# A hybrid encoder trunk: two gate blocks between the first two differential heads, and convolution taps dealt out differently

## The chip, the cores and the metric

The kernel runs on one core of a Trainium2 chip. The metric is the device time of one execution in microseconds (us); the median of several runs is given. The profile and the trace come from one further execution.

The engines go by short names: PE is TensorE (matrix products, with PEld for its weight loads), DVE is VectorE, ACT is ScalarE, POOL is GpSimd, SP is SyncE, which here only issues DMAs (copies between memories). SBUF is the working memory with 128 partitions, PSUM the memory into which PE writes.

## The reference

Two layers (DEPTH 2) over 512 tokens of width 1024, in float32. A layer computes three token mixers side by side from one normed input, merges them by gates, and goes on with a gated feed-forward part and a gated per-layer input:

```
h = rmsnorm(x, norm_mix[i])
proj = h @ w_in[i]
qa, ka, va, glu_in, qc, kc, vc, gates = split(proj)
ya = diff_attention(qa, ka, va, ...)          # 4 heads, two softmaxes each, rope on q and k
yb = conformer_conv(glu_in, ...)              # GLU, 31 taps per channel, layernorm, silu
yc = neighbourhood_attention(qc, kc, vc, rpb) # 8 heads, 8 x 16 window on an 8 x 64 grid
ga, gb, gc = split(sigmoid(gates))
merged = ga * (ya @ w_br_a[i]) + gb * (yb @ w_br_b[i]) + gc * (yc @ w_br_c[i])
x = x + merged @ w_o[i]
...                                           # feed-forward part, per-layer input
```

The convolution is one of 31 taps per channel over 512 channels, without mixing of channels: for each of four groups of 128 channels, 31 multiply-adds over a tile of 128 x 512.

## The kernel before

**Products.** Activations stand transposed, channels on the partitions and the 512 tokens along the row. Each float32 operand is split into a rounded high half (ACT, a copy into the type that PE multiplies) and the rest (DVE, a subtraction), `split` at L162. A product of 128 x 128 by 128 x 512 is three matmuls, high by high, high by low, low by high (`mm3`, L175). `gemm` (L181) runs one block: 8 of these, 24 matmuls. The weights of a block are one DMA of 512 KB on SP, a rounding on ACT and a subtraction on DVE (`weights`, L166), with three buffers for each.

**The order on PE is written by hand**: PE issues in the order in which the program names its instructions. Interleaving is done by ticks: four groups of three matmuls make a tick (`chunk`, L115), so a block of 24 matmuls is two ticks. `later` (L107) puts a unit of attention into a queue with a delay and a gap, both in ticks, and `tick` (L94) starts the queue's first entry as soon as both allow; a unit then continues itself some ticks later (its `yield`s).

**The other engines** issue in order too, but their order is made by the framework's scheduler, from the program order, priorities (the weights have a raised one) and its own estimate of times. SP's list of DMAs is made in the same way; an issue that waits holds up what stands behind it.

**A layer** (`layer`, L412) runs the GLU projections (`glu`), the four pairs of neighbourhood heads (`natten_in`, L624, with `natten_v` for the values) and the four differential heads (`diff_in`, L811, with `diff_v`, L840), with blocks of the gates between them (`gates`, L750: "c" is a block of the third gate, "b" one of the second); then `branch_c`, `merge_a`, the rest of the convolution (`conv`, L550), `merge_b`, `w_o`, the feed-forward part and `ple`.

- `natten_in` makes the two projections (query and key) of a pair, splits them and stacks the halves by DMA (`stack`, L649: 4 copies for the query, 8 for the key), and queues four units (`natten_unit`). A unit's products with the values go into the one PSUM bank of the tag `av`, from which `natten_y` is read (L747, L748).
- `diff_in` does the same for a head, with the rotation (rope) between: ACT copies the projection out of PSUM (`raw`), four DMAs on SP make the rotated copy (`rot`, L828), DVE multiplies both by the tables and adds them (L829 to L831, three steps), then the split and the stacking. It queues four units (`diff_unit`), whose first waits 8, 6, 6 or 7 ticks, by head. The fourth unit ends with a norm over the head's output, whose sums are read out of PSUM by a reduction (`norm`, L215).
- `gate_c` and `gate_b` run one block and copy it out of PSUM. The third gate's copies go to tiles of the tag `x`, which has four buffers and also holds one stacked key tile per pair and per head (`k2`).

**The taps.** The 124 multiply-adds of a layer's convolution are made one at a time by a generator (`taps`, L519). `background(after, n)` (L534) takes the next n of them and allows them behind the instruction `after`: n taps behind each gate block's copy, behind each low half of natten_in, behind each first rope step of diff_in, in branch_c (1 and 2 in turn) and in merge_a (4 behind the gate, 3 behind the addition, for each of 8 blocks). What is left is made at the start of `conv`, which then sums the four groups (`conv_ss`), splits the sum (`conv_qk`) and has PE add it over the channels (`conv_tr`, L564). The counts are in `BG` (L51) and in the calls of `layer`.

Of the kernel before, what the change touches and what calls it, by code (L numbers as in the profile page):

```python
# [11 lines left out]
F32 = mybir.dt.float32  # L12
# [3 lines left out]
ALU = mybir.AluOpType  # L16
# [31 lines left out]
PAR_L = 8 + 8 + 8 + 1 + 4 + 4 + 4 + 4 * CONV_W  # L48
PAR = L * PAR_L + 8
WARM = 9  # L50
BG = dict(glu=2, natten=3, diff=2, branchc=1, mergea=4, mergea2=3)  # L51
FIRST = (["v"] * 4 + ["pt"] * 2 + ["y", "b"], ["y"] * 5 + ["pt"] * 2 + ["b"])
GAP = 144
AHEAD = dict(sums=12, loads=10)
# [7 lines left out]
class Net:  # L62
# [98 lines left out]

    def split(self, hi, lo, src):  # L162
        self.act(hi, src, AF.Copy)
        self.tt(lo, src, hi.bitcast(F32), ALU.subtract)

    def weights(self, ap, n):  # L166
        with self.tc.high_priority(offset=min(self.w_ahead, self.tc.cur_priority - self.p0)):
# [123 lines left out]
    def build(self):  # L291
        nc, tc, a = self.nc, self.tc, self.a
        self.bufs = dict(wr=3, wh=3, wl=3, h=8, qk=2, kh=1, v=4, pt=2, y=5, z=5, x=4, t=7, rp=2,
                         e=2, a=3, r=3, ss=1, sm=8, rc=4, b=2, s=8)
        self.bg, self.w_ahead = BG, 400
        self.pbufs = dict(mm=3, sc=2, tr=2, av=1)
# [115 lines left out]
    def layer(self, i, h, xsrc, xs):  # L412
        self.i, self.h = i, h
        zs, cs = [], []
        self.todo = self.taps(zs, cs)
        self.glu(zs, range(3))
        yc, ya, yb = [], [], []
        acc, gb = [], []
        self.ms = iter(range(KD)), iter(range(KD))
        sn, sd = {}, {}  # L420
        self.natten_in(0, sn, yc)
        self.drain(self.renorm)
        if i == 0:
            self.lambdas()
        self.h = self.hs
        self.natten_v(sn)
        self.natten_in(1, sn, yc)
        finish = self.glu_last(zs)
        self.natten_in(2, sn, yc)
        self.gates(acc, gb, "cc", 2)  # L430
        self.natten_in(3, sn, yc)
        self.gates(acc, gb, "c", 2)
        self.diff_in(0, sd, ya)
        self.gates(acc, gb, "c", 2)
        self.diff_in(1, sd, ya)
        self.diff_v(sd)
        self.diff_in(2, sd, ya)
        self.gates(acc, gb, "bb", 3)
        self.diff_in(3, sd, ya)
        self.gates(acc, gb, "ccbbcc", 1)  # L440
        for g in acc + gb:
            self.act(g, g, AF.Sigmoid, table="sigmoid")
        finish()
        self.branch_c(acc, yc)
        self.merge_a(ya, acc)
        conv = self.run(self.conv(cs, yb))
        pairs = self.inputs()
        for m in range(4, KD):
            self.gate_b(gb, m, AF.Sigmoid, "sigmoid")
            for n in (((0, 1), (2,), (3, 4), (5,)), ((0,), (1,), (2,), (3,)))[i][m - 4]:  # L450
                self.input_block(pairs, n)
        self.drain(conv)
        mg = self.merge_b(yb, acc, gb)
        extra = self.extra_inputs(range(6 - 2 * i, 8 - 2 * i))
        x, h = self.w_o(mg, xsrc, extra)
        h = self.ffn(h, x, extra)
        return self.ple(h, x, xs, self.inputs() if i == L - 1 else None)
# [126 lines left out]

        yield from self.norm(st[0], CB, (3, 1), done)

    def values(self, ap, parts):

        mm = self.nc.tensor.matmul
        accs = [self.ps("mm") for _ in range(3)]  # L590
        ws = []

        def products(t, ks):
            ts = slice(t * P, (t + 1) * P)
            for k in ks:
                wh, wl = ws[k // 2]
                s = slice(k % 2 * 512, k % 2 * 512 + 512)
                hi, lo = self.halves(self.h[k])
                mm(accs[t], hi[:, ts], wh[:, s], start=k == 0, stop=False)
                mm(accs[t], hi[:, ts], wl[:, s], start=False, stop=False)  # L600
                mm(accs[t], lo[:, ts], wh[:, s], start=False, stop=k == KD - 1)
                self.chunk()

        for o in range(4):
            ws.append(self.weights(ap[:, o * 1024:(o + 1) * 1024], 1024))
        for ks in (range(2), range(2, 4)):
            for t in range(3):
                products(t, ks)
        for t in range(2):
            products(t, range(4, 6))  # L610
        accs.append(self.ps("av"))
        products(3, range(4))
        vs = []
        for t in range(2, 4):
            products(t, range(4, 6))
        for t in range(4):
            products(t, range(6, KD))
            v = self.sb("v", [P, 2, 512], F32R)
            for hi, lo, a in parts(v, accs[t]):
                self.split(hi, lo, a)  # L620
            vs.append(v)
        return vs

    def natten_in(self, pr, st, ys):  # L624

        self.phase = "natten"
        st4 = self.sb("qk", [P, 4, 512], F32R)
        k2 = self.sb("x", [P, 2, 512], F32R)
        nats = self.parts_of("kh", [512], 2, F32R)
        for s, off in enumerate((OFF_QC, OFF_KC)):  # L630
            ps = self.proj(off + pr * P)
            f = 1.0 if s else 0.125
            nat, low = nats[s], self.sb("t", [P, 512], F32R)
            if pr == 0:

                t = low.bitcast(F32)
                self.stt(t, ps, f, self.rb, ALU.mult, ALU.mult)
                ps, f = t, 1.0
            self.act(nat, ps, AF.Copy, scale=f)
            self.low = self.stt(low, ps, f, nat.bitcast(F32), ALU.mult, ALU.subtract)  # L640
            self.background(self.low, self.bg["natten"] if pr or self.i else 0)
            self.stack(nat, low, st4[:, 2 * s:2 * s + 2], k2 if s else None)
        box = {}
        ys.append(self.sb("y", [P, 2, 512], F32R))
        for n in range(4):
            self.later(self.natten_unit(pr, n // 2, n % 2, st4, k2, st, box, ys[pr]),
                       4 if pr else 6, 2)
# [163 lines left out]
    def diff_in(self, head, st, ys):  # L811
        self.phase = "diff"
        if head == 0:
            st["tabs"] = []
            for t in range(2):
                c = self.sb("r", [P, 512])
                self.nc.sync.dma_start(c, self.a["rope"][t])
                st["tabs"].append(c)
        st4 = self.sb("qk", [P, 4, 512], F32R)
        k2 = self.sb("x", [P, 2, 512], F32R)  # L820
        nats = self.parts_of("kh", [512], 2, F32R)
        for s, off in enumerate((OFF_QA, OFF_KA)):
            ps = self.proj(off + head * P)
            raw, rot = self.parts_of("rp", [512], 2)
            self.act(raw, ps, AF.Copy, scale=1.0 if s else 0.125)
            for b in range(4):
                o = b ^ 1
                self.nc.sync.dma_start(rot[32 * b:32 * b + 32], raw[32 * o:32 * o + 32])  # L828
            self.background(self.tt(raw, raw, st["tabs"][0], ALU.mult), self.bg["diff"])  # L829
            self.tt(rot, rot, st["tabs"][1], ALU.mult)  # L830
            self.tt(raw, raw, rot, ALU.add)  # L831
            nat, low = nats[s], raw.bitcast(F32R)
            self.split(nat, low, raw)
            self.stack(nat, low, st4[:, 2 * s:2 * s + 2], k2 if s else None)
        box = dict(s0=self.sb("sm", [P, 4]))
        for qt in range(4):
            self.later(self.diff_unit(head, qt, st4, k2, st, box, ys), (8, 6, 6, 7)[head],
                       1 if head == 3 else 2)

    def diff_v(self, st):  # L840
        self.phase = "diff"

        def parts(v, a):
            return [(v[:, :, 0:256], v[:, :, 256:], a.rearrange("p (g c) -> p g c", g=2))]

        st["v"] = self.values(self.a["w_va"][self.i], parts)

    def diff_unit(self, head, qt, st4, k2, st, box, ys):

# [689 lines left out]
```

## Time and profile before

| | |
|---|---|
| median of 3 runs | 1796.83 us (1796.43 to 1798.55) |
| the profiled execution | 1797.45 us |
| its span, first to last instruction | 1795.7 us |
| PE busy | 1771.4 us, 99% |
| DVE busy | 1372.6 us, 76% |
| ACT busy | 899.3 us, 50% |
| mean granted clock of PE | 0.997 |
| taps: conv_z, 128 x 512, 240 of them | 179.3 us, 747 ns each |

How to read the lines that follow. A line of the timeline has the start and the duration in us, the engine, the line of the kernel, the operation, the tile written and the tiles read, their sizes, and how many equal ones it merges (x3). In brackets stands how long the engine had been idle before and what ended that. A line of the waits has the engine that waited, its line, what it waited for, and then the total in us, the number of times and the longest. SPq is SP's queue of DMA issues. A line of the windows has the stretch, its length, the busy time of PE, PEld, DVE, ACT and POOL with the number of instructions, the granted clock of PE (1.00 is full), the share of the DMA engines and GB/s. Many operations are recorded under the line of a helper (L143 any ACT operation, L157 and L160 any DVE operation of two tensors), so the tile names tell them apart. Matmuls overlap: one takes 0.39 us from start to end, but the next starts 0.23 us later.

### The profile page before, as it was taken

The numbers are of one execution on the slowest core, as the hardware profiler recorded it, in microseconds if no ns is written. First come the engines' busy times: TensorE is split into PE (matmuls) and PEld (weight loads), VectorE is DVE, ScalarE is ACT, GpSimd is POOL, SyncE is SP. The second block draws the span as 40 slices with busy tenths as digits, with TensorE's granted clock in tenths as the row PEclk, the third lists the DMA queues.
The fourth block names the chain that finished last, engine by engine and source line by source line (L and its number), as shares of the span: only waits on it lengthen the run. The fifth ranks groups of instructions, "written<-read, shape, count | busy, mean of one in ns | idle before, by whom it ended". The sixth has DMA issues, their size and how long they took to land.

```text
span 1795.7 us, 26536 instructions
## 1 busy us (share of the span) xinstructions
PE 1771.4 (99%) x10019; PEld 1551.3 (86%) x10019; DVE 1372.6 (76%) x2113; ACT 899.3 (50%) x1480; POOL 63.6 (4%) x102
## 2 busy tenths in 40 slices
PE   9999999999999999999999999999999999999998
PEld 7888788887899899898888887888888998998987
DVE  7678787897887667577786787879978775775776
ACT  5556555425565345254545665463255652542544
POOL 0000000000000000000000000000000100000000
PEclk9999999999999999999999999999999999999999
DMA  5666543333746456243437664433354662763432
GB/s 191 188 188 161 139 125 93 101 99 119 227 136 178 151 142 187 107 139 109 161 107 199 173 179 129 127 85 99 108 184 153 183 198 72 190 179 108 121 109 95
DMA packets 98384, 257.51 MB, mean 143 GB/s; under 512 B 12880, under 2 KB 17616, under 8 KB 98256
## 3 DMA queue, kind: packets, MB, share of 16 engines
q1 hardware_dynamic: 90912, 231.00, 41.2%
q0 software_dynamic: 6336, 23.07, 7.1%
q8 instruction: 79, 1.29, 0.3%
q10 hardware_dynamic: 1008, 1.75, 0.3%
q14 instruction: 49, 0.40, 0.1%
HBM read 216.44 MB, written 7.86 MB: 125 GB/s over the span
## 4 chain that ended last, share of the span: by engine, by line
PE 89%; DVE 7%; DMA 2%; issue 1%; ACT 1%; SPq 0%; POOL 0%; DVEq 0%; POOLq 0%; ACTq 0%
PE ffn_sc L1101 14%; PE ffn_av L1101 7%; PE ffn_mm L178 4%; PE ffn_mm L179 4%; PE ffn_mm L177 4%; PE ffn_tr L1101 4%; PE mergea_mm L178 2%; PE mergea_mm L177 2%; PE mergea_mm L179 2%; DVE conv_z L160 2%; PE wo_mm L178 2%; PE wo_mm L177 2%; PE wo_mm L179 2%; PE natten_mm L177 1%; PE natten_mm L178 1%; PE natten_mm L179 1%
## 5 line engine op out<-in xcount | busy, mean ns | idle before, releaser
L143 ACT ACTIVATE ffn_wh<-ffn_wr 128x1024 fp32r<-128x1024 f32 (+1 forms) x114 | 117.3, 1029 | 183.2 <-PE ffn_mm L178 105.7
L160 DVE SCALAR_TENSOR_TENSOR conv_z<-glu_z,pre_par,conv_z 128x512 f32<-128x512 f32 x240 | 179.3, 747 | 2.8
L157 DVE TENSOR_TENSOR ffn_wl<-ffn_wr,ffn_wh 128x1024 fp32r<-128x1024 f32 (+1 forms) x114 | 135.0, 1184 | 43.3 <-ACT ffn_wh L143 42.8
L1101 PE MATMUL ffn_sc<-wo_h,ffn_wh 128*128 128x256 f32 x704 | 130.4, 283 | 0.0
L1101 PEld LDWEIGHTS ffn_sc<-wo_h,ffn_wh 128*128 128x128 f32 x704 | 110.4, 192 | 0.8
L1101 PE MATMUL ffn_sc<-wo_h,ffn_wl 128*128 128x256 f32 x352 | 99.6, 283 | 0.0
L177 PE MATMUL ffn_mm<-ffn_z,ffn_wh 128*128 128x512 f32 x240 | 93.4, 389 | 0.0
L178 PE MATMUL ffn_mm<-ffn_z,ffn_wh 128*128 128x512 f32 x240 | 93.4, 389 | 0.0
L179 PE MATMUL ffn_mm<-ffn_z,ffn_wl 128*128 128x512 f32 x240 | 93.4, 389 | 0.0
L157 DVE TENSOR_TENSOR ffn_t<-ffn_mm,wo_r 128x512 f32<-128x512 f32 x48 | 33.1, 689 | 75.3 <-PE ffn_mm L179 75.3
L157 DVE TENSOR_TENSOR ffn_wl<-ffn_rp,ffn_wh 128x1024 fp32r<-128x1024 f32 x44 | 53.8, 1222 | 30.1 <-ACT ffn_wh L143 30.1
L143 ACT ACTIVATE mergea_wh<-mergea_wr 128x1024 fp32r<-128x1024 f32 (+1 forms) x32 | 27.1, 847 | 88.8 <-PE mergea_mm L178 80.4
L1101 PEld LDWEIGHTS ffn_sc<-wo_h,ffn_wl 128*128 128x128 f32 x352 | 67.5, 192 | 0.0
L1101 PE MATMUL ffn_sc<-wo_qk,ffn_wh 128*128 128x256 f32 x352 | 67.1, 283 | 0.0
L1101 PE MATMUL ffn_sc<-wo_v,ffn_wh 128*128 128x256 f32 x352 | 67.1, 283 | 0.0
L1101 PE MATMUL ffn_av<-wo_h,ffn_wh 128*128 128x256 f32 x352 | 65.3, 283 | 0.0
L143 ACT ACTIVATE ffn_wh<-ffn_rp 128x1024 fp32r<-128x1024 f32 x44 | 46.4, 1055 | 29.4 <-PE ffn_mm L178 17.5
L1101 PEld LDWEIGHTS ffn_sc<-wo_qk,ffn_wh 128*128 128x128 f32 x352 | 54.9, 192 | 0.0
L1101 PEld LDWEIGHTS ffn_av<-wo_h,ffn_wh 128*128 128x128 f32 x352 | 54.9, 192 | 0.0
L1101 PEld LDWEIGHTS ffn_sc<-wo_v,ffn_wh 128*128 128x128 f32 x352 | 54.9, 192 | 0.0
L906 DVE TENSOR_REDUCE diff_s<-diff_sc 128x1 f32<-128x512 f32 x64 | 42.6, 684 | 14.9 <-PE diff_sc L809 14.8
L179 PEld LDWEIGHTS ffn_mm<-ffn_z,ffn_wl 128*128 128x128 f32 x240 | 45.1, 188 | 9.3
(726 smaller groups left out, 5639.7 us busy)
## 6 DMA issues: line engine op xcount, KB each, us to landing
ffn_wr<-w_gu SPq DMA_DIRECT2D x66, 512.0 KB, 4.3
ffn_e<-w_gu SPq DMA_DIRECT2D x32, 512.0 KB, 3.7
ffn_e<-w_gu POOLq DMA_DIRECT2D x32, 512.0 KB, 7.9
ffn_wr<-w_fd SPq DMA_DIRECT2D x32, 512.0 KB, 4.7
natten_wr<-w_in SPq DMA_DIRECT2D x16, 512.0 KB, 4.2
natten_b<-bias SPq DMA_DIRECT2D x32, 256.0 KB, 4.2
gatec_wr<-w_in SPq DMA_DIRECT2D x16, 512.0 KB, 4.4
diff_wr<-w_in SPq DMA_DIRECT2D x16, 512.0 KB, 4.3
```

What stands on the lines that cost most here:

```text
L143: i = self.nc.scalar.activation(out, in_, func, **kw)
L157: return self.nc.vector.tensor_tensor(out, a, b, op)
L160: return self.nc.vector.scalar_tensor_tensor(out, a, s, b, op0, op1)
L177: mm(out, wh, ah, start=first, stop=False)
L178: mm(out, wh, al, start=False, stop=False)
L179: mm(out, wl, ah, start=False, stop=last)
L906: nc.vector.tensor_reduce(out=m[:, u:u + 1], in_=sc, op=ALU.max, axis=AX.X, negate=True)
L1101: mm(bank[:, u], w[:, u, kp], t, start=begin and n == 0, stop=False, skip_group_check=True)
```

## The change

In `layer`, one block of the third gate moves from ahead of `diff_in(0)` to behind it, so two stand between heads 0 and 1, and head 0's units wait 10 ticks in place of 8. The taps are dealt out anew: behind each projection of `natten_in` 4 in layer 1 and 5 in layer 0 (none for pair 0 there) in place of 3; behind each first rope step 1 in place of 2; behind the two "b" blocks 2 in place of 3; and one behind each of the four splits of the differential values, where there was none. `split` returns its DVE instruction for that. No arithmetic changes.

```
-BG = dict(glu=2, natten=3, diff=2, branchc=1, mergea=4, mergea2=3)
+BG = dict(glu=2, diff=1, branchc=1, mergea=4, mergea2=3)
...
     def split(self, hi, lo, src):
         self.act(hi, src, AF.Copy)
-        self.tt(lo, src, hi.bitcast(F32), ALU.subtract)
+        return self.tt(lo, src, hi.bitcast(F32), ALU.subtract)
...
         self.natten_in(3, sn, yc)
-        self.gates(acc, gb, "c", 2)
         self.diff_in(0, sd, ya)
-        self.gates(acc, gb, "c", 2)
+        self.gates(acc, gb, "cc", 2)
         self.diff_in(1, sd, ya)
         self.diff_v(sd)
         self.diff_in(2, sd, ya)
-        self.gates(acc, gb, "bb", 3)
+        self.gates(acc, gb, "bb", 2)
         self.diff_in(3, sd, ya)
...
-    def values(self, ap, parts):
+    def values(self, ap, parts, taps=0):
...
             for hi, lo, a in parts(v, accs[t]):
-                self.split(hi, lo, a)
+                self.background(self.split(hi, lo, a), taps)
...
-            self.background(self.low, self.bg["natten"] if pr or self.i else 0)
+            self.background(self.low, 4 if self.i else 5 * (pr > 0))
...
-            self.later(self.diff_unit(head, qt, st4, k2, st, box, ys), (8, 6, 6, 7)[head],
+            self.later(self.diff_unit(head, qt, st4, k2, st, box, ys), (10, 6, 6, 7)[head],
                        1 if head == 3 else 2)
...
-        st["v"] = self.values(self.a["w_va"][self.i], parts)
+        st["v"] = self.values(self.a["w_va"][self.i], parts, 1)
```

## The prediction

> **What bounds the kernel now.** First the page: engines, then the queue that PE runs in order.
>
> ```profile
> span 1795.7 us, 26536 instructions
> PE 1771.4 (99%) x10019; PEld 1551.3 (86%) x10019; DVE 1372.6 (76%) x2113; ACT 899.3 (50%) x1480; POOL 63.6 (4%) x102
> ```
> PE is busy for 1771.4 us of 1795.7. It issues in an order written by hand, the change takes no matmul away, so all that can be won is in the 24.3 us in which PE stands still and in matmuls that run slow. The view of waits of PE lists who ends those pauses (total us, times, longest):
>
> ```profile
> PE diff_tr L863 <- DVE diff_sm L215: 5.0, 4, 1.3
> PE conv_tr L564 <- ACT conv_qk L143: 4.4, 1, 4.4
> PE natten_av L741 <- DVE natten_y L157: 2.3, 2, 1.4
> PE diff_av L599 <- DVE natten_y L157: 1.9, 2, 1.0
> ...
> PE diff_sc L809 <- ACT diff_a L143: 0.9, 2, 0.5
> ```
> Together 14.5 us, and each lies where this change moves work: in the differential heads (diff, natten_av), or where the convolution must be complete (conv_tr). VectorE (DVE) is named, directly or one step back, in all. So I looked at each place in the timeline of DVE.
>
> The largest, in layer 0, by DVE, ACT and PE in turn:
>
> ```profile
> 409.19 2.32 DVE L160 SCALAR_TENSOR_TENSOR conv_z<-glu_z,pre_par,conv_z 128x512 f32<-128x512 f32 x3
> 411.43 1.22 DVE L157 TENSOR_TENSOR gateb_wl<-gateb_wr,gateb_wh 128x1024 fp32r<-128x1024 f32 x1
> 412.56 0.75 DVE L160 SCALAR_TENSOR_TENSOR conv_z<-glu_z,pre_par,conv_z 128x512 f32<-128x512 f32 x1
> 413.34 0.69 DVE L157 TENSOR_TENSOR conv_ss<-conv_ss,conv_z 128x512 f32<-128x512 f32 x1
> ```
> ```profile
> 410.14 1.06 ACT L143 ACTIVATE gateb_wh<-gateb_wr 128x1024 fp32r<-128x1024 f32 x1 [3.98 <-PE gateb_mm L178]
> 411.11 0.58 ACT L143 ACTIVATE gateb_v<-gateb_mm 128x512 f32<-128x512 f32 x1
> 414.07 0.63 ACT L143 ACTIVATE conv_qk<-conv_ss 128x512 fp32r<-128x512 f32 x1 [2.38 <-DVE conv_ss L157]
> ```
> ```profile
> 414.75 1.52 PE L564 MATMUL conv_tr<-conv_qk,pre_onesr 128*128 128x512 f32 x2 [4.42 <-ACT conv_qk L143]
> ```
> The last four taps shown, a weight split among them, stand ahead of the sum conv_ss (413.34); ACT rounds it (414.07), PE starts 0.68 later. PE had finished at 414.75 - 4.42 = 410.33. The pause has a second price, in the windows view (the column after POOL is the granted clock):
>
> ```profile
> 413.50:414.70 1.20, 0.00 (x0) 0.00 (x0) 0.54 (x1) 0.63 (x1) 0.00 (x0) 0.53 0.32 109
> 414.70:420.40 5.70, 5.65 (x13) 4.15 (x14) 4.71 (x8) 3.07 (x6) 0.00 (x0) 0.50 0.01 4
> ```
> By 413.50, 3.2 us after the last matmul, the clock has all but fallen to half, and the first 5.70 us of PE's work run at 0.50: half of 5.70, 2.85 us, is lost again. The stall costs 4.4 + 2.85 = 7.25 us. [...]
>
> **The change, part by part.** *Counting taps.* Each layer has 4 x 31 = 124. From the code, layer 0 before: 6 projections x 3 = 18 behind natten (pair 0 has none), 16 behind diff, 20 behind the gate blocks, 12 in branch_c: 66; merge_a takes 56, and 2 are left for conv. After: 6 x 5 = 30, 8, 18, 12, and 4 behind the values: 72; merge_a takes the last 52. Layer 1: 76 before merge_a and 48 in it become 78 and 46. So layer 0 loses 6 taps exactly at the end: the 2 left over, the 3 behind the last addition, one of the 4 behind the last gate.
>
> ```profile
> L160 DVE SCALAR_TENSOR_TENSOR conv_z<-glu_z,pre_par,conv_z 128x512 f32<-128x512 f32 x240 | 179.3, 747 | 2.8
> ```
> 6 x 0.747 = 4.48 us. With DVE working through to 413.34, conv_ss moves to about 408.9, ACT's rounding to 409.6 and PE's start to 410.3: the very moment at which PE arrives. What could hold it is the weight split at 411.43, which waits for ACT's at 410.14, which waits for PE: if these stay ahead, see the first rival. Layer 1, whose taps already end early, shows the order that I expect: sum, rounding, and only then the weights.
>
> ```profile
> 1294.31 0.69 DVE L157 TENSOR_TENSOR conv_ss<-conv_ss,conv_z 128x512 f32<-128x512 f32 x1
> ```
> ```profile
> 1295.45 0.62 ACT L143 ACTIVATE conv_qk<-conv_ss 128x512 fp32r<-128x512 f32 x1
> 1297.41 1.06 ACT L143 ACTIVATE gateb_wh<-gateb_wr 128x1024 fp32r<-128x1024 f32 x1 [1.35 <-issue]
> ```
> The row of conv_tr counts one wait, layer 0's, so layer 1 has none there. **Term: -4.4 and -2.85.** What is late next in layer 0 is the product after it, whose weights are split from 410.14 on; PE needs them behind the 13 matmuls that took 5.70 us at half clock, so 2.85 at full clock: at 413.2. They are there at 411.43 + 1.22 = 412.65. Covered by 0.5 us; a split that comes later than that costs PE the excess.
>
> *One tap less behind each rotation.* The wait of diff_tr, four times alike:
>
> ```profile
> 238.53 0.16 DVE L911 RECIPROCAL diff_s<-diff_s 128x1 f32<-128x1 f32 x1 [0.55 <-ACT diff_e L143]
> ...
> 242.66 0.74 DVE L160 SCALAR_TENSOR_TENSOR conv_z<-glu_z,pre_par,conv_z 128x512 f32<-128x512 f32 x1
> 243.32 0.68 DVE L157 TENSOR_TENSOR diff_rp<-diff_rp 128x512 f32<-128x512 f32 x1
> 243.92 0.68 DVE L215 TENSOR_REDUCE diff_sm<-diff_tr 128x4 f32<-128x512 f32 x1
> ```
> ```profile
> 244.66 0.66 PE L863 MATMUL diff_tr<-pre_ident,diff_a 128*128 128x128 f32 x4 [1.25 <-DVE diff_sm L215]
> ```
> The transposes need a PSUM buffer that the reduction L215 frees. The reduction is ready long before and stands in DVE's queue behind a rotation's steps and their two taps; the run begins at 238.53, held by ACT, so a tap saved before that changes nothing and one saved behind it moves L215 by 0.66 (242.66 to 243.32). The change leaves one of the two. 1.25 becomes 0.59, four times: **-2.6** (bounds: 0, if the scheduler fills the place with something else; -5.0, if ACT comes earlier too).
>
> *The swapped block.* Layer 0's natten stage in three windows, the third being diff_in(0), two blocks of 24 matmuls with the natten units between them (columns: PE, PEld, DVE, ACT, POOL):
>
> ```profile
> 101.10:128.30 27.20, 27.20 (x144) 23.19 (x144) 20.10 (x47) 17.56 (x42) 0.45 (x3) 1.00 0.62 175
> 128.30:149.40 21.10, 21.10 (x116) 18.19 (x115) 18.07 (x41) 13.91 (x34) 0.45 (x3) 1.00 0.56 150
> 149.40:163.50 14.10, 14.10 (x78) 12.16 (x77) 9.08 (x22) 9.24 (x23) 0.30 (x2) 1.00 0.68 180
> ```
> One gate block that stood between the last natten_in and diff_in(0) goes behind it, so diff_in(0) runs 14.10 / 2 = 7.05 us earlier. All that it issues comes earlier by that: on SP two weight loads, eight rotation copies, twelve stacking copies; on ACT two copies and two roundings; on DVE six rope steps, two splits. On POOL it issues nothing. The gate block's one load, one copy, one split and its two taps go later. The two also swap their turns for the four x buffers; each gets one that natten pairs 1 and 2 have done with before, so nothing waits. Since the delay of head 0's units grows from 8 to 10 ticks, and a block is two ticks, their matmuls stand where they stood; from diff_in(1) on PE's order is the old one.
>
> What this meets: head 0's rope now sits on the heels of the gate block's taps and collides with the last natten units.
>
> ```profile
> 165.11 0.69 DVE L157 TENSOR_TENSOR diff_rp<-diff_rp,diff_r 128x512 f32<-128x512 f32 x1 [1.18 <-DMA diff_rp<-diff_rp]
> ...
> 178.90 0.73 DVE L160 SCALAR_TENSOR_TENSOR conv_z<-glu_z,pre_par,conv_z 128x512 f32<-128x512 f32 x1
> ...
> 181.77 0.42 DVE L157 TENSOR_TENSOR natten_y<-natten_y,natten_av 64x256 fp32r<-64x256 f32 x1
> ```
> ```profile
> 182.34 0.71 PE L741 MATMUL natten_av<-natten_pt,natten_v 128*128 128x256 f32 x4 [1.39 <-DVE natten_y L157]
> ```
> From 165.11 to 182.19 DVE has no pause, and the read of the av bank (natten_y, 181.77) ends 1.4 us after PE wanted to write it. Afterwards the first rope step starts near 165.11 - 7.05 = 158.1, where DVE has room (third window), two taps are gone from the ropes, and the gate blocks' two (178.90 is one) come behind them: 4 x 0.66 = 2.6 us less ahead of natten_y, against 1.4 and 0.9 missing. **-2.3** (bounds 0 and -2.3).
>
> ```profile
> 202.11 0.42 DVE L157 TENSOR_TENSOR natten_y<-natten_y,natten_av 64x256 fp32r<-64x256 f32 x1
> ```
> ```profile
> 202.67 0.47 PE L599 MATMUL diff_av<-diff_wh,glu_h 128*128 128x512 f32 x1 [0.97 <-DVE natten_y L157]
> ```
> The next two waits are the same lag one head later: natten_y comes only at 202.11, which I read as head 1's ropes standing in front of it, late because their copies sat on SP behind head 0's. With SP free of these 7 us earlier, and two taps fewer: **-2.8** (1.9 + 0.9; bounds 0 and -2.8).
>
> *What pays for it.* Idle on DVE in the three windows above: 7.1, 3.0 and 5.0. The eight extra taps of natten_in(2) and (3) are 8 x 0.747 = 6.0 against 10.1 in the first two windows; the moved rope steps take most of the third, less the gate taps that leave it. It fits on average, not everywhere: one unit of natten may come late in each layer. I put back **+2.3**, the size of the two natten_av waits (bounds 0 and 4.4, the largest wait there is). The four taps behind the differential values I take at nothing, since the list has no wait of PE for what DVE makes of the values; at worst they are 4 x 0.66 = 2.6 us per layer, inside the third rival's price per tap.
>
> SP issues in order too, and a rotation copy that waits for ACT holds the weight loads behind it:
>
> ```profile
> 157.56 1.20 SPq L828 DMA_DIRECT2D diff_rp<-diff_rp  x2
> ```
> From here to the first rope step (165.11, after 1.18 us of waiting for the copies) it is 7.5 us. It will be so again, one block earlier, and now right behind the last natten pair's stacking copies. None of the waits listed names a weight, so the loads have a lead; I cost this at nothing, and if the lead is gone a load costs what it is late, at most those 7.05 us once per layer.
>
> **Sum.** -4.4 - 2.85 - 2.6 - 2.3 - 2.8 + 2.3 = -12.65. The profiled execution took 1797.45 us (1.75 outside the span); the median of the runs is 1796.83. So 1784.8 by the former, 1784.2 by the latter; I give 1784.2.
>
> **Rivals.**
>
> *The convolution's wait stays in part.* For it: in layer 0 the weights' rounding (410.14) stands ahead of conv_qk on ACT. If it still does, conv_qk starts at 411.11 + 0.58 = 411.69 and PE at 412.4: 2.0 us of pause, under the 3.2, so the clock holds: 1786.2. If the split at 411.43 also stays ahead, conv_ss waits for 412.56, PE for 413.97: 3.6 us, and the clock falls: 1784.2 + 3.6 + 2.85 = 1790.7. Against it: layer 1's order.
>
> *The waits only move.* PE is at 99%, DVE's total is unchanged, no work is removed; each tap not done here is done there, and PE, in order, meets the same lag elsewhere: 1796.8. [...] Against it: idle DVE time in the windows above, and a layer 1 that has no conv wait with only four taps fewer in merge_a than layer 0 will have. Also here: that the scheduler, which orders DVE by its own estimate, delays taps that are merely allowed earlier.
>
> *Slower: the natten units fall behind.* A unit comes every 7.05 us and its av must wait until natten_y of the one before has been read. If DVE's lag exceeds what is left of a period, each further tap is PE's delay. Twelve extra taps in layer 0 and eight in layer 1, 20 x 0.747 = 14.9 us, all of it on PE; the two natten lags (2.3 and 2.8) are not won, 7.25 and 2.6 are: 1796.8 + 14.9 - 9.85 = 1801.9. It decides where a stretch of natten has less DVE idle than its new taps; in the second window, 3.0 against 4 x 0.747 = 3.0, it is a tie. Against it: before, PE waits for natten's reads only where the ropes collide with them, not in the windows that get the taps.
>
> **How the numbers follow.** Forecast 0.70, first rival 0.12, second 0.10, third 0.08. The forecast's own range is 1779.5 (the bounds: 2.4 more at diff_tr, 2.3 not put back) to 1789 (4.4 put back, one of the diff terms missing). With the first rival up to its 1790.7, and a little for a scheduler that I cannot run, 1779 to 1792 leaves out the other two. A difference of 0.2%, 3.6 us, is about what a measurement here can tell from none. Faster by more than that: forecast and first rival, 0.82; same 0.10; slower 0.08.
>
> **What would show it.** Right: conv_tr gone from PE's waits in layer 0 and the granted clock at 1.00 from 410 to 420; diff_tr's four waits near 0.6 each; natten_av and diff_av below 1 us in all; first rope step of head 0 near 158. Wrong: conv_ss still behind a weight split; new PE waits of natten_av, natten_tr or natten_mm between 100 and 165 us or in layer 1's like stretch; a matmul waiting for a weight split behind the moved copies.

## The result and the profile after

The changed kernel takes 1781.74 us (median of 4 runs, 1781.65 to 1781.94) against 1797.30 (4 runs, 1796.43 to 1798.55) for the kernel before on the same chip: ratio 0.9913, interval 0.9896 to 0.9930. That is 15.6 us less, where 12.65 were forecast (1784.2 us, counted from 1796.83). The profiled execution took 1781.65 us, its span is 1779.9. From its page:

```profile
PE 1767.4 (99%) x10019; PEld 1551.4 (87%) x10019; DVE 1372.7 (77%) x2113; ACT 897.9 (50%) x1480; POOL 63.5 (4%) x102
```

DVE has the same work; PE's busy time falls by 4.0 us with the same matmuls, and its idle time from 24.3 to 12.5. The waits of PE (total us, times, longest):

```profile
PE diff_av L177 <- DVE diff_v L157: 2.8, 2, 1.4
PE pre_av L325 <- DVE pre_zeror L382: 1.1, 1, 1.1
PE ple_tr L213 <- DVE ple_ss L157: 1.0, 1, 1.0
PE natten_mm L598 <- DVE natten_t L160: 0.8, 1, 0.8
PE natten_av L741 <- issue: 0.5, 1, 0.5
PE conv_tr L226 <- POOL conv_rc L222: 0.4, 1, 0.4
```

All five lines that the prediction showed are gone, and two are new: diff_av for the low half of the values, and natten_av L741. (From L432 on, lines stand one earlier than before.) Four places of the changed kernel's timeline: the rope of head 0 and the read of the av bank, the values, a reduction L215, the convolution's end.

```profile
160.14 0.69 DVE L157 TENSOR_TENSOR diff_rp<-diff_rp,diff_r 128x512 f32<-128x512 f32 x1 [0.28 <-DMA diff_rp<-diff_rp]
...
198.98 0.42 DVE L157 TENSOR_TENSOR natten_y<-natten_y,natten_av 64x256 fp32r<-64x256 f32 x1
...
214.91 0.74 DVE L160 SCALAR_TENSOR_TENSOR conv_z<-glu_z,pre_par,conv_z 128x512 f32<-128x512 f32 x1
215.57 1.28 DVE L905 TENSOR_REDUCE diff_s<-diff_sc 128x1 f32<-128x512 f32 x2
216.77 0.68 DVE L157 TENSOR_TENSOR diff_v<-diff_av,diff_v 128x512 fp32r<-128x512 f32 x1
217.60 0.36 PE L177 MATMUL diff_av<-diff_pt,diff_v 128*128 128x256 f32 x1 [1.39 <-DVE diff_v L157]
...
240.03 0.68 DVE L215 TENSOR_REDUCE diff_sm<-diff_tr 128x4 f32<-128x512 f32 x1
240.63 0.68 DVE L157 TENSOR_TENSOR diff_rp<-diff_rp 128x512 f32<-128x512 f32 x1
...
400.52 0.69 DVE L157 TENSOR_TENSOR conv_ss<-conv_ss,conv_z 128x512 f32<-128x512 f32 x1
401.25 0.63 ACT L143 ACTIVATE conv_qk<-conv_ss 128x512 fp32r<-128x512 f32 x1 [0.24 <-DVE conv_ss L157]
...
405.54 0.62 PE L563 MATMUL conv_tr<-conv_qk,pre_onesr 128*128 128x512 f32 x2
```

To be seen: the rope begins at 160.14 (165.11 before); the read of the av bank that ended a wait at 202.11 comes at 198.98; a tap (214.91) stands ahead of the low half for which PE waits 1.39 us; L215 stands ahead of the last rope addition, behind which it stood before; and conv_qk's first half is ready at 401.88, 3.66 us ahead of PE. The windows show the clock unbroken there:

```profile
405.00:410.00 5.00, 5.00 (x24) 4.12 (x23) 3.81 (x6) 3.66 (x6) 0.00 (x0) 1.00 0.17 47
410.00:420.00 10.00, 10.00 (x50) 8.28 (x49) 6.30 (x12) 5.36 (x11) 1.01 (x1) 1.00 0.56 173
```

PE's order being the same outside the swapped block, the start of one and the same matmul in both traces tells where the time went. The third column is the shift, the last how much of it came since the row above.

| matmul | before | after | shift | change |
|---|---|---|---|---|
| natten_sc, ahead of the last units of layer 0 | 177.70 | 178.46 | +0.76 | +0.76 |
| first diff_tr | 211.86 | 208.81 | -3.05 | -3.81 |
| second group of diff_tr, behind the values | 227.27 | 225.49 | -1.78 | +1.27 |
| gateb_mm, behind two L215 | 281.83 | 277.16 | -4.67 | -2.89 |
| gateb_mm, behind conv_tr and its successor | 420.84 | 408.74 | -12.10 | -7.43 |
| natten_sc of layer 1, ahead of its last units | 1070.48 | 1059.29 | -11.19 | +0.91 |
| gateb_mm, layer 1, behind the values | 1124.40 | 1111.05 | -13.35 | -2.16 |
| gateb_mm, layer 1, behind two L215 | 1174.49 | 1158.69 | -15.80 | -2.45 |

From there to the end nothing changes. The +0.76 is there at the first GLU product already (33.56 and 34.34), ahead of all that the change touches. The pauses cost more than their length here: around the last natten units of layer 0 three of 2.69 us in all went (1.39, 0.33, 0.97), and 3.81 us of time. Of the other 1.12 us, 0.48 is overlap: in an unbroken run a matmul starts 0.23 us behind the one before it, which lasts 0.39, so 0.16 us beside each pause lie under the end of the matmul ahead of it. Most of what is left lies at the four matmuls of diff_sc behind the pause of 0.33: they start 0.34 us apart in the kernel before (200.30 to 201.31) and 0.23 apart here (198.82 to 199.50).

### The profile page after: what moved, and what is told of

The parts are those of the page before. It is cut to its first block, busy times and chain, and to the rows that moved or that the text cites. A ratio compares the mean times of both kernels' runs of the same rounds, so it can differ in the third digit from the quotient of the medians.

```text
span 1779.9 us, 26531 instructions
## 1 busy us (share of the span) xinstructions
PE 1767.4 (99%) x10019; PEld 1551.4 (87%) x10019; DVE 1372.7 (77%) x2113; ACT 897.9 (50%) x1480; POOL 63.5 (4%) x102
## 4 chain that ended last, share of the span: by engine, by line
PE 96%; DVE 2%; issue 1%; DMA 0%; ACT 0%; SPq 0%; POOL 0%; POOLq 0%; DVEq 0%; ACTq 0%
PE ffn_sc L1100 14%; PE ffn_av L1100 7%; PE ffn_mm L177 4%; PE ffn_mm L178 4%; PE ffn_mm L179 4%; PE ffn_tr L1100 4%; PE mergea_mm L179 2%; PE mergea_mm L177 2%; PE mergea_mm L178 2%; PE wo_mm L178 2%; PE wo_mm L179 2%; PE wo_mm L177 2%; PE gateb_mm L178 2%; PE gateb_mm L179 2%; PE gateb_mm L177 2%; PE natten_mm L177 1%
```

## The experiments

The theory after reading the two traces: each pause has a cause of its own, the gain at the convolution comes from the six taps, that at diff_tr from a changed order of DVE, that at the natten units from the swapped block. The rivals: one lag of DVE that the swap, or the dealing of taps, cures alone. Times are medians; each ratio is to the kernel before on the same chip, whose medians were 1798.63 us (the swap, the taps, and the taps at the convolution's end), 1798.10 (the rope's taps and the first three runs on the values) and 1798.56 (the last three). The expectations of the first group count from 1797.0, so 1.6 us too low for its chip.

**Each half alone.** The swap, with the taps as before (in `layer` and the delay):

```
-        self.gates(acc, gb, "c", 2)
         self.diff_in(0, sd, ya)
-        self.gates(acc, gb, "c", 2)
+        self.gates(acc, gb, "cc", 2)
...
-(8, 6, 6, 7)[head],
+(10, 6, 6, 7)[head],
```

> The kernel before with the gate block moved behind head 0 and the delay of 10 ticks; every count of taps as before. Theory (each pause of PE has a cause of its own): the waits of natten_av (2.3 us), of the old diff_av (1.9) and of diff_sc (0.9) go, since the ropes of head 0 start 7 us earlier; conv_tr keeps its 4.4 us and the clock its 0.50 behind it, diff_tr keeps four waits of about 1.25, and no new wait of diff_av comes. 1797.0 - 5.1 = 1792 (1790.5 to 1794). Rival 1 (one lag: the ropes are late because DVE carries two taps behind each of them, so that the swap alone does nothing): natten_av and diff_av stay, 1797. Rival 2 (the order that the scheduler gives DVE round the reduction L215 comes from the moved block): diff_tr's four waits go here as well, 1787.

Measured: 1791.88 us, 0.9966 (0.9953 to 0.9978). PE's waits with the swap alone:

```profile
PE diff_tr L862 <- DVE diff_sm L215: 5.0, 4, 1.3
PE conv_tr L563 <- ACT conv_qk L143: 4.4, 1, 4.4
...
PE diff_sc L808 <- ACT diff_e L143: 1.0, 2, 0.6
```

The two waits for natten_y are gone (4.2 us), diff_sc's is not, and the other waits stand as before. The theory's time holds, and the swap does win something by itself: by the starts of the matmuls in the table above, 2.64 us at the natten units of layer 0 and 2.44 in layer 1. A further 0.87 us at the convolution belong to the clock: behind the same pause of 4.4 us the granted clock is 0.50 from 413.01 to 416.42 and 1.00 after that, in the kernel before it is 0.50 for twice as long. Then the new taps, in the old order of blocks: the changed kernel with the two lines above undone.

> The changed kernel with the old place of the gate block and the old delay of 8 ticks: only the taps are dealt out anew. Theory (causes apart): conv_tr's 4.4 us go and the clock stays at 1.00 (2.85 more), diff_tr's four waits (5.0) go, the wait of diff_av for the values' low half stands as in the changed kernel (2.8), and natten_av and diff_av for natten_y stay at some 2.3 to 5 us: 1797.0 - 4.4 - 2.85 - 5.0 + 2.8 = 1787.6 (1786 to 1790). Rival 1 (the waits only move while the ropes sit on the last natten units): natten_av and diff_av for natten_y grow by the taps added behind natten, to 8 us or more, 1791 or more. Rival 2 (the swap is what the change lives on): conv_tr goes but diff_tr stays, 1792 to 1793.

Measured: 1782.21 us, 0.9911 (0.9898 to 0.9925): the whole gain, with no block moved. Of the waits round the edited places this is the one left that counts:

```profile
PE diff_av L177 <- DVE diff_v L157: 3.5, 2, 1.8
```

The waits for natten_y are gone here too. The theory missed: it kept 2.3 to 5 us for them. Swap and taps each cure them, so the swap has nothing left to win.

**Which taps matter at the natten units and at diff_tr.** One tap in place of two behind each rope step, nothing else; the eight taps per layer fall to the end:

```
-BG = dict(glu=2, natten=3, diff=2, branchc=1, mergea=4, mergea2=3)
+BG = dict(glu=2, natten=3, diff=1, branchc=1, mergea=4, mergea2=3)
```

> The kernel before with one tap behind each first rope step in place of two, and nothing else: the eight taps per layer go to the end of merge_a. Read place by place. Theory (DVE's order decides at diff_tr: with one tap less the scheduler puts the reduction L215 ahead of the last rope addition, two steps earlier instead of one): all four waits of diff_tr go, 5.0 us. Rival A (the step of my prediction): they shrink to 0.6 each, 2.4 in all. For the neighbourhood units: natten_av, diff_av and diff_sc (5.1 us together) go with the ropes' taps alone, as they did with all the taps dealt anew; rival B: they need the swapped block or the taps behind natten, and stay. At conv_tr in layer 0 the eight taps add 8 x 0.747 = 6.0 to the pause of 4.4, to 10.4, with two or three stretches of half clock; in layer 1, where conv_qk is ready 6 us ahead of PE, they add nothing to 1. Sum: 1798 - 5.0 - 5.1 + 6.0 + 1.0 = 1795 (theory); 1797.5 with rival A, 1800 with rival B, 1802 with both.

Measured: 1798.37 us, 1.0000 (0.9991 to 1.0009). A null in the sum, where the theory's sum was 1795, but not place by place. The waits:

```profile
PE conv_tr L564 <- ACT conv_qk L143: 13.4, 2, 10.7
...
PE diff_av L177 <- DVE diff_v L157: 0.6, 2, 0.3
...
PE diff_tr L863 <- DVE diff_sm L215: 0.2, 1, 0.2
PE natten_av L742 <- DVE natten_a L157: 0.2, 1, 0.2
```

```profile
238.06 0.69 DVE L157 TENSOR_TENSOR diff_rp<-diff_rp,diff_r 128x512 f32<-128x512 f32 x1
238.66 0.69 DVE L215 TENSOR_REDUCE diff_sm<-diff_tr 128x4 f32<-128x512 f32 x1
239.26 0.69 DVE L157 TENSOR_TENSOR diff_rp<-diff_rp 128x512 f32<-128x512 f32 x1
```

The timeline shows L215 ahead of the last rope addition, as in the changed kernel, and diff_tr's 5.0 us shrink to 0.2: the theory, not the prediction's 0.59 each. The natten waits are gone with this one number. At the end the eight taps cost 6.3 us in layer 0 and 2.7 in layer 1, where the expectation had at most 1, and half clock on top.

**The taps at the convolution's end.** Six more taps early in layer 0, in `natten_in`, with the ropes as before:

```
-            self.background(self.low, self.bg["natten"] if pr or self.i else 0)
+            self.background(self.low, (3 if self.i else 4) if pr or self.i else 0)
```

> The kernel before with one tap more behind each projection of natten pairs 1 to 3 in layer 0 (4 in place of 3), and nothing else: six taps fewer are left at the end of merge_a. Theory: conv_tr waits no more in layer 0 and the granted clock stays at 1.00 behind it, -4.4 - 2.85 = -7.25; all other waits stay (diff_tr 5.0, natten_av 2.3, diff_av 1.9, diff_sc 0.9): 1789.8 (1789 to 1791.5). Rival 1 (the weight split gateb_wl stays ahead of conv_ss): a pause of 2 to 3.6 us is left, 1792 to 1796. Rival 2 (each further tap behind natten is PE's delay): natten_av grows by up to 6 x 0.75 = 4.5 us and eats the gain, 1794.

and three of them, behind the key alone (`3 + s` in place of 4):

> The kernel before with one tap more behind the key projection alone of natten pairs 1 to 3 in layer 0 (3 and 4 in place of 3 and 3): three taps fewer at the end of merge_a. Theory (the taps at the end set the start of conv_ss, and the clock falls at a threshold): the pause of conv_tr shrinks by 3 x 0.747 to 2.2 us, and being shorter than 3.2 it leaves the clock at 1.00: -2.2 - 2.85 = -5.1, 1791.9. Rival 1 (the loss of clock grows with the pause): half of each, -2.2 - 1.4, 1793.4, with a clock below 1.00 in the 5 us behind the pause. Rival 2 (DVE has its order from the weights, not from the taps): the sum conv_ss comes much earlier once a few taps are gone, no pause is left, 1789.8, as with six taps fewer.

Measured: 1792.28 us, 0.9967 (0.9954 to 0.9979), and 1795.14, 0.9983 (0.9974 to 0.9992). With six, conv_tr's wait is gone and nothing waits there; but the added taps cost PE something new, which rival 2 had foreseen, though at another wait:

```profile
PE natten_av L742 <- DVE natten_a L157: 1.9, 1, 1.9
```

In the changed kernel, with a tap less behind the ropes, natten carries even more taps and this wait is absent. With three, the pause is 2.3 us in two parts, where the count gave 2.2:

```profile
PE conv_tr L564 <- ACT conv_qk L143: 1.4, 1, 1.4
...
PE conv_tr L564 <- DVE conv_qk L157: 0.8, 1, 0.8
```

The pause is not linear in the taps: with none fewer it is 4.42, with three 2.3, and with six not 4.42 - 4.48, about nothing, but a lead of 3.66 (411.37 - 407.71). With six fewer the scheduler puts conv_ss ahead of steps behind which it stood before (the two of pin_e, the gate's split), as in the changed kernel.

**What halves the clock.** At the convolution both runs win about what their theories say, by the starts of the same matmuls: 7.46 us with six taps (7.25 expected), 4.64 with three (5.1). They lose elsewhere: 1.31 us at the natten units of layer 0 with six, where the wait of 1.9 is new and others shrink, and 2.03 us in layer 1 with three, where one wait of natten_av grows by 0.5 us and no wait explains the rest. The windows do; cut at the clock's own edges, they show for the run with six, in layer 0, and the run with three, in layer 1:

```profile
195.55:198.96 3.41, 1.53 (x9) 1.21 (x9) 3.35 (x7) 0.68 (x2) 0.00 (x0) 1.00 0.54 127
198.96:202.38 3.42, 3.42 (x9) 2.63 (x8) 3.25 (x8) 1.89 (x5) 0.00 (x0) 0.50 0.63 144
```

```profile
409.40:412.81 3.41, 1.97 (x8) 1.11 (x6) 2.76 (x4) 2.06 (x3) 0.00 (x0) 1.00 0.08 32
412.81:416.22 3.41, 2.57 (x12) 2.13 (x12) 2.82 (x6) 1.22 (x3) 0.00 (x0) 1.00 0.19 43
...
1088.65:1092.06 3.41, 1.90 (x7) 1.05 (x7) 3.25 (x8) 1.97 (x6) 0.00 (x0) 1.00 0.65 152
1092.06:1095.48 3.42, 3.42 (x10) 2.65 (x9) 2.16 (x6) 1.83 (x3) 0.00 (x0) 0.50 0.67 155
```

Here a window of 3.41 us in which PE was idle for 1.88 (3.41 - 1.53) or 1.51 us is followed by one at half clock, which costs half of 3.41, 1.7 us. The second fence holds the sharpest pair: 1.44 us idle left the clock alone, 1.51 halved it, and those 1.51 are two pauses that the kernel before has too, of 0.54 and 0.97; there an edge at 1092.81, 199 windows of 3.4133 us behind the fall at 413.56, parts them:

```profile
413.56:416.97 3.41, 2.22 (x5) 1.49 (x6) 1.83 (x4) 0.63 (x1) 0.00 (x0) 0.50 0.13 43
416.97:420.39 3.42, 3.42 (x10) 2.65 (x9) 3.36 (x7) 3.07 (x6) 0.00 (x0) 0.50 0.01 2
...
1089.40:1092.81 3.41, 2.99 (x14) 2.12 (x13) 3.41 (x7) 1.72 (x5) 0.00 (x0) 1.00 0.39 91
1092.81:1096.23 3.42, 2.33 (x8) 1.42 (x9) 3.26 (x8) 1.52 (x5) 0.00 (x0) 1.00 0.78 180
```

The same fence shows the stall of the kernel before as two windows at half clock, of which the first was partly idle.

**The taps behind the differential values.** The changed kernel without them (`parts, 1` back to `parts` in `diff_v`), the four taps left to the end; then with them behind the values of the neighbourhood heads (`parts, 1` in `natten_v`), in the new and in the old order of blocks:

> The changed kernel without the tap behind each split of the differential values; those four taps go to the end of merge_a. Theory: the wait of diff_av for the values' low half (2.8 us, half in each layer) goes, and the whole change would have been worth that much more; but in layer 0 the four taps come back at the end, where six fewer gave a lead of 3 us and three fewer a pause of 2.3: with two fewer than before a pause of about 2.9 us at conv_tr, with or without a stretch of half clock (1.7). 1781.7 - 2.8 + 2.9 = 1781.8 (1780.5 to 1784). Rival 1 (PE must wait at diff_av whatever stands behind the values): diff_av keeps its 2.8 us, 1784.6. Rival 2 (a linear count: six taps gave 4.4 + 3.0 us, so two give 2.5 and the lead is taken up smoothly): conv_tr waits 2 us, 1781.

> The changed kernel with the taps behind the differential values moved to the values of the neighbourhood heads (one behind each of those eight splits, in a stretch where DVE stands idle for a third of the time), so that four taps fewer than in the changed kernel are left at the end. Theory: the wait of diff_av (2.8 us) goes, nothing comes in its place, conv_tr does not wait: 1781.7 - 2.8 = 1778.9 (1778 to 1780), faster than both kernels. Rival (each tap ahead of a read of PSUM is PE's delay somewhere): a wait of natten_av or natten_sc of the first pair comes instead, 1780 to 1783.

> The same dealing of taps as the run before this one, but with the gate block in its old place ahead of head 0 and the old delay of 8 ticks. Theory (with one tap behind each rope the natten units are no longer late, so the swap has nothing left to win): the same time as with the swapped block, 1778.9, within 0.5 us, with no wait of natten_av. Rival (the swap takes the ropes off the last natten units): natten_av and diff_av wait 1 to 5 us, 1780 to 1784.

Measured: 1784.07 us, 0.9920 (0.9907 to 0.9934), at the upper end of the theory's range; 1783.30, 0.9919 (0.9905 to 0.9932); 1783.18, 0.9919 (0.9907 to 0.9932). The first lost its 2.8 us at diff_av and got these, from its waits and its windows:

```profile
PE conv_tr L563 <- ACT conv_qk L143: 1.9, 1, 1.9
PE diff_av L598 <- DVE natten_y L157: 1.0, 1, 1.0
...
PE conv_tr L563 <- DVE conv_qk L157: 0.5, 1, 0.5
```

```profile
405.26:408.67 3.41, 1.03 (x4) 0.61 (x4) 2.85 (x4) 1.94 (x3) 0.00 (x0) 1.00 0.04 5
408.67:412.08 3.41, 3.41 (x10) 2.63 (x9) 2.63 (x5) 1.92 (x4) 0.00 (x0) 0.50 0.14 41
```

A pause of 2.4 us at conv_tr, in one window, is followed by a window at half clock, which costs 1.7 us more. So the first rival of the prediction, which took 2.0 us of pause to leave the clock alone, could have erred. The second run missed the theory by 4.4 us; its rival named what came instead and was 0.3 us short. These are its new waits, beside 0.7 us of diff_av for natten_y:

```profile
PE natten_av L741 <- DVE natten_a L157: 1.5, 3, 0.7
PE natten_av L740 <- DVE natten_pt L157: 1.3, 1, 1.3
```

DVE's idle share there says little: the new taps stand in front of what PE needs next. The third took the same time in the old order of blocks.

**The same taps, one place later.** All four behind the last of the four splits, in the new and in the old order, and the changed kernel once more on the same chip:

```
-                self.background(self.split(hi, lo, a), taps)
+                self.background(self.split(hi, lo, a), taps * (t == 3))
...
-        st["v"] = self.values(self.a["w_va"][self.i], parts, 1)
+        st["v"] = self.values(self.a["w_va"][self.i], parts, 4)
```

> The changed kernel with all four taps that it puts behind the differential values behind the last of the four splits, so that none stands ahead of a low half that PE waits for; every other count is the same, and so is the number of taps left at the end. DVE stands idle for 3.3 us right behind that place in the changed kernel, room for four taps of 0.66. Theory (the wait of diff_av comes from the taps that stand in front of the last low half, not from their number): diff_av's 2.8 us go, at most 0.3 per layer are left, nothing takes their place: 1781.7 - 2.8 = 1778.9 (1778.3 to 1780), faster than both kernels. Rival (four taps in the stretch of the values are DVE's lag wherever they stand): diff_pt, diff_sc or diff_tr of the next units come late instead, 1780.5 to 1782.

> The same dealing as the run before this one, with the gate block in its old place and the old delay. Theory (the swapped block is worth nothing once the ropes carry one tap): within 0.7 us of the run before this one, 1779 to 1780. Rival (the swap is worth something where nothing else waits): 1 us or more slower.

> The changed kernel once more, on the same chip and against the same runs of the kernel before as the two runs ahead of it. All theories: 1781.5 to 1782, with the two waits of diff_av of 1.39 us each.

Measured: 1780.13 us (1778.72 to 1781.09), 0.9898 (0.9883 to 0.9913), 0.1 above the theory's range; 1779.04 (1778.87 to 1779.68), 0.9893 (0.9878 to 0.9908); 1782.08 (1781.37 to 1782.28), 0.9909 (0.9892 to 0.9925). In the new order:

```profile
214.85 0.68 DVE L905 TENSOR_REDUCE diff_s<-diff_sc 128x1 f32<-128x512 f32 x1
215.45 0.68 DVE L157 TENSOR_TENSOR diff_v<-diff_av,diff_v 128x512 fp32r<-128x512 f32 x1
216.05 0.74 DVE L160 SCALAR_TENSOR_TENSOR conv_z<-glu_z,pre_par,conv_z 128x512 f32<-128x512 f32 x1
216.28 0.36 PE L177 MATMUL diff_av<-diff_pt,diff_v 128*128 128x256 f32 x1
```

The low half comes at 215.45, the taps behind it, and the wait of diff_av is gone from the list. The time falls by 1.95 us against the changed kernel in this group (1782.08), of the 2.8 expected; the spans of the two profiled executions, 1776.9 and 1780.2, are further apart, but the former was the fastest of its four runs. The same number of taps in the same stretch, behind the value that PE needs instead of ahead of it, is faster than both kernels: no run of it reaches the fastest of the changed kernel. The old order of blocks is, if anything, 1.1 us faster still, past the 0.7 that the theory allowed and on the other side than the rival: the swap wins nothing here either.

## Why the prediction was right, and where not

*The convolution, -4.4 and -2.85:* measured -7.43 at that place, so the term is right in size, and the six taps alone do it (-7.46). Its picture is not: conv_qk is not ready at "the very moment at which PE arrives" but 3.66 us before, since the order round conv_ss changed as well. The size did not suffer, because a lead wins no more than a pause that just closes. The first rival's order did not come: ACT rounds conv_ss at 401.25 and the gate's weights at 405.56. "By 4.48 us" is a count of taps in a fixed order, and the order is not fixed. The margin of 0.5 us for the next product's weights held: nothing waits there.

*The half clock:* the loss was read rightly, its rule not. It is no threshold of 3.2 us of pause: 1.51 us of idle time in a window were enough. And the 5.70 us of work at half clock are no length of their own: with the swap alone, behind the same pause, the clock is back 3.41 us after its fall (413.01 to 416.42). The traces fit a clock that changes at the edges of a grid. In the kernel before it falls at 413.56 and rises at 420.39, 6.83 us and so two windows on; it falls again near the end, in this window of the kernel before,

```profile
1792.40:1792.60 0.20, 0.00 (x0) 0.00 (x0) 0.00 (x0) 0.00 (x0) 0.00 (x0) 0.87 0.00 0
```

whose mean of 0.87 puts the edge 0.74 of the way through it, at 1792.55: 1378.99 us after the first fall, into which half of 6.83 goes 403.8 times, so 404 windows of 3.4133 us. Half of 3.41, 1.7 us, is the price of one window, and the kernel before paid two, the first in part.

*diff_tr, -2.6:* mis-sized; -5.0 of pauses, -5.34 by place. The failed step is "one saved behind it moves L215 by 0.66": with one tap the scheduler also puts L215 ahead of the last rope addition, as the run with one rope tap alone shows. The bound of -5.0 was there, for another reason (ACT).

*natten_av, diff_av and diff_sc, -2.3 and -2.8:* all gone, the size of the pauses right, the cause not. The prediction gave them to the swapped block, with two taps as help. The swap by itself removes 4.2 us of pauses, the tap by itself nearly all, and beside the tap the swap is worth nothing: without it and with it 0.9911 and 0.9913 of the kernel before, 1783.18 and 1783.30 us, 1779.04 and 1780.13. The two causes are one lag, counted once and rightly, but the change needed only one of its halves. The rope's first step came at 160.14, not 158.1.

*Put back, +2.3:* a wait of 0.48 (natten_av L741, layer 1; the list names no cause, but 0.10 us ahead of its end DVE ends natten_a, which stands behind a tap), +0.91 by place. The heavier load does cost a wait of 1.9 us where the ropes keep two taps; with one it nearly fits, and the third rival's lag did not come.

*Four taps behind the values, nothing:* wrong, by 2.8 us of waits and 2.54 by place. The failed step is its reason, "the list has no wait of PE for what DVE makes of the values". The list names pauses from 0.15 us on, and a value that is missing from it need not have room. The timeline of the kernel before shows that there was none:

```profile
218.56 0.68 DVE L157 TENSOR_TENSOR diff_v<-diff_av,diff_v 128x512 fp32r<-128x512 f32 x1
218.87 0.39 PE L179 MATMUL diff_mm<-glu_h,diff_wl 128*128 128x512 f32 x1
219.38 0.36 PE L177 MATMUL diff_av<-diff_pt,diff_v 128*128 128x256 f32 x1
```

The low half ends at 219.24 and PE uses it 0.14 us later. That is no lead: in the changed kernel, where PE waits 1.39 us for the same value, it is 0.15 (217.45 and 217.60), and it is 0.14 to 0.15 in both layers of all thirteen profiles. PE's matmul before it ends at 219.26, so PE was already waiting, for 0.12 us. The three taps that stand ahead of the value (the fourth stands behind it) make this 1.39 us; the 1.27 on top are the table's +1.27. The second rival, waits that only move, was right in this one place.

*SP and the moved copies, nothing:* held; no wait of PE names a DMA.

By place, with the values of layer 1 taken at layer 0's +1.27: diff_tr won 2.74 more than forecast, the natten units 2.14 more (7.24 for pauses of 5.1, which cost more than their length), the convolution 0.18 more, and 1.39 less was to be put back; the values cost 2.54 more, and 0.76 came from the start. That is 3.15 us between the forecast's -12.65 and the span's -15.80: the sum was near because errors of both signs met, not because each step was right.

## What to carry to other kernels

Before background work is put behind an instruction, look in the timeline at how far ahead of its reader that result is made, not at whether a list of waits names it: three taps ahead of a value that had no lead at all cost 1.39 us of waiting in each layer, and right behind it the taps cost none. Where a scheduler orders an engine, one instruction less can reorder its neighbours, so a count of instructions gives a term's sign and a first size, and only the order that the built kernel's trace shows gives its size. When a change has two halves that attack the same wait, build each alone: here one of them carried all of it.

## What the runs showed of the hardware

Short pauses halved the clock in these runs. In the thirteen profiles, from the first GLU product to 25 us ahead of the end, with edges counted in steps of 3.4133 us from a fall of the same profile, a window of 3.41 us at full clock was followed by a fall where PE was idle in it for 1.51, 1.59, 1.88, 2.38 us and more (eight times), and never where it was idle for 1.44 or less; one window with 1.76, in the run with the taps alone (214.79 to 218.20), had no fall, so the idle time alone does not decide.

The grid does not start with the kernel: counted from the start of the span, the edge at 413.56 us lies at 121.16 windows in the kernel before, the edge at 198.96 at 58.29 in the run with six taps. So the same two pauses, 0.54 and 0.97 us, cost 1.7 us in one kernel's execution and nothing in another's. This fits the spread of the kernel before, 1796.64 to 1799.89 us over the 15 runs of the first group, about the price of two windows. In those runs the time goes with the mean granted clock: 1796.64 to 1797.81 us in the five with 0.999, 1798.17 to 1799.89 in the six with 0.997. Which pauses took the clock from them is not shown, since these runs left no trace.
